# Where two token blocks take their first RMS norms from, and how far the attention's projections run ahead

## The chip, the core and the metric

The kernel runs on one core of one Trainium2 chip. The core has five queues of instructions that run beside each other: TensorE (PE in the profile, with its weight loads as PEld), VectorE (DVE), ScalarE (ACT), GpSimd (POOL) and SyncE (SP), which in this kernel issues all the DMA transfers. An engine works through its own queue in order and waits for others by semaphores. The metric is the device time of one execution in microseconds (us), the median over runs.

## The reference

One transformer layer, batch 1, 2048 tokens, width 1024, 16 heads of 64: an adaptive RMS norm, stick-breaking attention, a gated residual, a second adaptive norm, and a SwiGLU network of width 2816. Everything is float32. The part that the change touches is the first norm and what it feeds:

```python
def rms_norm(x, g):
    xf = x.astype(jnp.float32)
    y = xf * lax.rsqrt(jnp.mean(xf * xf, axis=-1, keepdims=True) + EPS)
    return (y * g.astype(jnp.float32)).astype(x.dtype)
...
    h = modulate(rms_norm(x, norm_g[i, 0]), sh_m, sc_m)
    y = stick_breaking_mixer(h, w_qkv, w_o)
...
    # in the mixer: causal blocks; softplus, a reversed running sum, exp
    qkv = (h @ w_qkv).reshape(b, s, 3, N_HEADS, HEAD_DIM)
    z = jnp.einsum('bthd,bshd->bhts', q[:, q0:end], k[:, :end]).astype(jnp.float32) * scale
    rest = lax.cumsum(jnp.where(mask, jax.nn.softplus(z), 0.0), axis=3, reverse=True)
    a = jnp.exp(jnp.where(mask, z - rest, -jnp.inf)).astype(v.dtype)
```

So each token needs one number, the reciprocal root of its mean square over the 1024 features; the features are then scaled, shifted and multiplied with the weights for Q, K and V.

## The kernel before

**Tiling.** The 2048 tokens are four blocks of 512 (b = 0 to 3), the 16 heads are eight pairs (p = 0 to 7), the 1024 features are KC = 8 chunks of 128. Products run in split precision: each operand is a high and a low float32r part, and one 128x128 by 128x512 product is three matmuls (`mm3`, L198 to L200). TensorE needs the normalised block with features on the partitions, `ht` (L415 to L423 write its two parts); it is also stored to DRAM (`h_s`), since later pairs load it from there.

**Projections.** A step is one (pair, block), in the order of `STEPS`: (0,0) and (1,0) first, woven together by hand, then (0,1), (0,2), (0,3), (1,1) and so on. Each later step is a generator `project` (L472) that computes K, then Q, then V (t = 1, 0, 2), eight products each, one per *slice*; with two empty slices a step has 26. After K and Q the result is split into two parts in a `qkn` buffer and moved by DMAs into `kt` and `qt`. The step (1,0) is *parked*: its K and Q are split into two `wraw` buffers and go by DMA to DRAM (`k_park`, `q_park`), to be fetched when pair 1 begins. There are two `wraw` buffers, three `qt`, seven `kt`, seven `v` and four `tmp` buffers, and three accumulator banks (`acc`) in PSUM.

**What sets the order.** The instructions of PE, ACT, DVE and POOL stand in the order in which the program text emits them; SP's DMAs are placed by the framework's scheduler. The attention runs in *slots*, four to a unit of (pair, head, query block, key block): in a slot PE multiplies one score tile `z`, ACT makes two sigmoids of an older one (L627, L629), DVE runs the product scan (L639, L644), POOL multiplies (L651), PE transposes (L661), and ACT and DVE split the result (L671, L677) for the product with V (L689). Between these stands a number of projection slices. `AHEAD` says how many slices are to be done by slot 11; the first slot comes after `AHEAD - EAGER` of them (30 and 12 make 18), and `RATE` spreads the rest of the 780 slices evenly over the attention's weighted slots.

**The first norm.** Block 0 is normalised by tokens: `x_load` puts 128 tokens a tile, ACT squares them with a sum (L189), DVE and POOL make the reciprocal root (L191, L193), DVE scales (L389), PE transposes four 128x128 pieces per chunk (`x_turn`, L395), ACT applies gain and shift. Blocks 1 to 3 come from `xt`, a copy of x that the host has laid out with features on the partitions (`cols_load`, L325: four tiles `xc` of two chunks). Block 1's mean squares are still taken by tokens, from a second load. Blocks 2 and 3 take them from the columns: ACT squares the four tiles (`cols_square`, L341), POOL and DVE add them up (L347, L349), PE sums over the partitions by four products with a column of ones (`cols_sum`, L355, into `xq`), DVE and POOL make the root (L359, L361). Four spread tiles (L369) are then transposed into a row over the tokens (`x_share`, L376), ACT copies it (`xv`, L381), and the columns are multiplied by it and the gain: even chunks on DVE (L404), odd ones on POOL (L408). `first_norm` (L435) does this three chunks ahead of the product that needs it. The table `X_AT` says at which (step, t, k) the pieces are emitted; `x_do` maps its words to functions.

Of the kernel before, what the change touches and what calls it, by code (L numbers as in the profile page):

```python
# [44 lines left out]
AHEAD = 3 * KC + 6  # L45
# [26 lines left out]

X_AT = {
    (2, 1, 1): [("load", 3)],
    (2, 1, 3): [("square", 2, 0)],
    (2, 1, 4): [("square", 2, 1), ("add", 2, 1)],
    (2, 1, 5): [("square", 2, 2)],
    (2, 1, 6): [("square", 2, 3), ("add", 2, 2)],
    (2, 1, 7): [("add", 2, 3)],
    (2, 0, 0): [("add", 2, 4)],  # L80
    (2, 0, 5): [("sum", 2)],
    (2, 0, 6): [("spread", 2)],
    (2, 2, 0): [("share", 2)],
    (2, 2, 3): [("square", 3, 0)],
    (2, 2, 5): [("square", 3, 1)],
    (2, 2, 7): [("add", 3, 1)],
    (3, 1, 0): [("square", 3, 2)],
    (3, 1, 2): [("add", 3, 2)],
    (3, 1, 3): [("square", 3, 3)],
    (3, 1, 5): [("add", 3, 3)],  # L90
    (3, 1, 6): [("add", 3, 4)],
    (3, 0, 1): [("sum", 3)],
    (3, 0, 2): [("spread", 3)],
    (3, 0, 6): [("share", 3)],
}

ON_GPSIMD = ((2, 1), (3, 1), (3, 2))
# [29 lines left out]
def hybrid_trunk_kernel(  # L127
# [25 lines left out]
    nc.vector.memset(lead, -0.5)  # L153
# [160 lines left out]
    x_pairs, x_squares, x_spreads = {}, {}, {}  # L314

    def x_load(b, i, tag="v"):
        tok = att.tile([P, D], F32, name=f"x{b}_{i}", tag=tag, bufs=BUFS[tag])
        r0 = b * BT + i * P
        nc.sync.dma_start(tok, x[r0 : r0 + P])
        x_tiles[b, i] = tok  # L320

    def cols_load(b, *which, tag="kt"):
        for m in which or range(KC // 2):
            cols = att.tile([P, 2, BT], F32, name=f"xc{b}_{m}", tag=tag, bufs=BUFS[tag])
            nc.sync.dma_start(cols, xt[b - 1, :, 2 * m : 2 * m + 2])  # L325
            x_pairs[b, m] = cols
            x_cols[b, 2 * m], x_cols[b, 2 * m + 1] = cols[:, 0], cols[:, 1]

    def x_square(b, i):
        junk = x_tiles[b, i]  # L330
        if b == 0:
            junk = x_norm[i] = att.tile([P, D], F32, name=f"xn0_{i}", tag="kt", bufs=BUFS["kt"])
        x_rstd[b, i] = rms_scale(att, x_tiles[b, i], f"n0_{b}_{i}", junk=junk)

    def cols_square(b, m):
        if m == 0 or (m == 2 and b == 2):
            both = att.tile([P, 2, 2, BT], F32, name=f"xs{b}_{m}", tag="qt", bufs=BUFS["qt"])
            x_squares.setdefault(b, []).extend([both[:, 0], both[:, 1]])
        elif m > 1 and b == 3:
            x_squares[b].append(x_squares[b][1])  # L340
        nc.scalar.activation(x_squares[b][m], x_pairs.pop((b, m)), AF.Square)  # L341

    def cols_add(b, m):
        total = x_squares[b][0]
        if m < KC // 2:
            engine = nc.gpsimd if (b, m) in ON_GPSIMD else nc.vector
            engine.tensor_tensor(total, total, x_squares[b][m], op=ALU.add)  # L347
        else:
            nc.vector.tensor_tensor(total[:, 0], total[:, 0], total[:, 1], op=ALU.add)  # L349

    def cols_sum(b):
        total = x_squares.pop(b)[0]
        ps = accps.tile([P, BT], F32, name=f"xq{b}", tag="acc")
        for i in range(4):
            nc.tensor.matmul(  # L355
                ps[:, i : i + 1], total[:, 0, i * P : (i + 1) * P], ones[:, 0:1], start=True, stop=True
            )
        ms = att.tile([P, 4], F32, name=f"xm{b}", tag="x_ms", bufs=1)
        nc.vector.tensor_scalar(ms, ps[:, :4], 1.0 / D, EPS, op0=ALU.mult, op1=ALU.add)  # L359
        rstd = att.tile([P, 4], F32, name=f"xd{b}", tag="x_rstd", bufs=1)  # L360
        nc.gpsimd.tensor_tensor(rstd, ms, lead[:, :4], op=ALU.pow)  # L361
        x_rstd[b] = rstd

    def x_spread(b, *which):
        if b not in x_spreads:
            x_spreads[b] = att.tile([P, 4, P], F32, name=f"xw{b}", tag="tmp", bufs=BUFS["tmp"])
        for i in which or range(4):
            rstd = x_rstd[b][:, i : i + 1] if b > 1 else x_rstd.pop((b, i))
            nc.vector.tensor_scalar(x_spreads[b][:, i], ones, rstd, None, op0=ALU.mult)  # L369

    def x_share(b):
        spread = x_spreads.pop(b)
        pool, tag = (tps, "t") if b < 2 else (accps, "acc")
        pt = pool.tile([P, BT], F32, name=f"xr{b}", tag=tag)
        for i in range(4):
            nc.tensor.transpose(pt[:, i * P : (i + 1) * P], spread[:, i], ident)  # L376
        if b == 1:
            x_row[b] = pt
            return
        x_row[b] = att.tile([P, BT], F32, name=f"xv{b}", tag="tmp", bufs=BUFS["tmp"])  # L380
        nc.scalar.copy(x_row[b], pt)  # L381

    x_do = {
        "load": cols_load, "square": cols_square, "add": cols_add, "sum": cols_sum,
# [3 lines left out]
    def x_scale(i):  # L388
# [380 lines left out]
    def turn_x(m):  # L769
        turned_x[m] = x_turn(m)  # L770
# [1033 lines left out]
```

## Time and profile before

| | us |
|---|---|
| median of 3 runs | 2848.14 (2847.87 to 2855.06) |
| the profiled execution's own time | 2851.93 |
| its span, first to last instruction | 2849.8 |
| PE busy in the span | 2802.1 (98%) |
| DVE busy | 2027.4 (71%) |
| ACT busy | 1633.5 (57%) |
| POOL busy | 1289.5 (45%) |

The span holds the whole program: an opening of some 65 us in which weights, x and the modulation arrive, the first projections and the start of the attention until about 150 us, the attention with its projections until about 1450 us, and then the output projection and the network. "Busy" of PE counts modelled ends of pipelined matmuls: two 128x512 matmuls of 0.39 us each that start 0.23 us apart run at full rate. The granted clock (PEclk) is the share of its full clock that TensorE was given. A row such as `L395 MATMUL xT<-begin,xn ... x4` reads: line 395, tile `xT` written from `begin` and `xn`, four of them. Names in lists of the program's order carry numbers of their buffers; in the profile these are left out.

### The profile page before, as it was taken

What the parts mean: (1) busy time and instruction counts of PE and PEld (TensorE: products, weight loads), DVE (VectorE), ACT (ScalarE), POOL (GpSimd) and SP (SyncE); (2) the same over time, 40 slices, a digit from 0 to 9 for tenths busy, and PEclk for the clock granted to TensorE, in tenths of its full rate; (3) what the DMA queues carried; (4) which work ended last, traced back from release to release, by engine and by line L of the source; (5) the groups of instructions that cost most, each with busy time, mean ns of one, the idle gap of its engine ahead of it and who ended that gap; (6) DMA issues with size and microseconds to landing.
All of it is one profiled execution on the core that took longest, in us unless ns stands there. A gap on an engine that the chain in (4) does not pass through costs nothing.

```text
span 2849.8 us, 41730 instructions
## 1 busy us (share of the span) xinstructions
PE 2802.1 (98%) x13809; PEld 2334.5 (82%) x13809; DVE 2027.4 (71%) x2828; ACT 1633.5 (57%) x3268; POOL 1289.5 (45%) x2033
## 2 busy tenths in 40 slices
PE   9799999999999999999999999999999999999999
PEld 6688888888888888887887888888888888888887
DVE  7688898888888888888866866655776655124366
ACT  5587777788787777877645533333433333322243
POOL 1575666666576655657410222222222222544454
PEclk9899999999999999999999999999999999999999
DMA  9765647657565545637289645334553335545575
GB/s 361 251 211 165 198 140 243 197 174 236 173 221 198 188 138 170 211 117 243 69 304 308 214 137 159 111 92 153 159 168 117 111 98 172 191 133 153 181 225 192
DMA packets 239209, 518.94 MB, mean 182 GB/s; under 512 B 22417, under 2 KB 108433, under 8 KB 222098
## 3 DMA queue, kind: packets, MB, share of 16 engines
q1 hardware_dynamic: 238994, 516.28, 55.8%
q8 instruction: 109, 1.79, 0.3%
q14 instruction: 106, 0.87, 0.1%
HBM read 348.95 MB, written 118.49 MB: 164 GB/s over the span
## 4 chain that ended last, share of the span: by engine, by line
PE 86%; DVE 4%; DMA 3%; issue 2%; ACT 2%; POOL 1%; SPq 0%; DVEq 0%; POOLq 0%; ACTq 0%
PE s L198 9%; PE s L200 9%; PE s L199 9%; PE z L610 8%; PE o L689 8%; PE t L661 8%; PE pj L198 5%; PE pj L199 5%; PE pj L200 5%; PE o L199 5%; PE o L198 5%; PE o L200 5%; PE y L200 1%; PE y L198 1%; PE y L199 1%
## 5 line engine op out<-in xcount | busy, mean ns | idle before, releaser
L651 POOL TENSOR_TENSOR a<-a,w 128x512 f32<-128x512 f32 (+3 forms) x640 | 622.7, 973 | 219.5 <-DVE w L644 129.0
L644 DVE TENSOR_TENSOR_SCAN w<-z,c,begin 128x512 f32<-128x512 f32 x384 | 489.6, 1279 | 83.4 <-ACT z L629 61.9
L198 PE MATMUL s<-r,l 128*128 128x512 f32 x1232 | 481.5, 391 | 1.2 <-DVE p L1535 0.7
L200 PE MATMUL s<-r,l 128*128 128x512 f32 x1232 | 479.6, 389 | 0.0
L199 PE MATMUL s<-r,l 128*128 128x512 f32 x1232 | 479.4, 389 | 0.0
L627 ACT ACTIVATE a<-z 128x512 f32<-128x512 f32 (+3 forms) x640 | 347.1, 542 | 168.1 <-PE z L610 137.7
L689 PE MATMUL o<-aT,v 128*128 128x512 f32 (+3 forms) x1280 | 385.0, 382 | 0.1
L677 DVE TENSOR_TENSOR aT<-t,aT 128x512 fp32r<-128x512 f32 (+3 forms) x640 | 359.1, 595 | 23.7 <-ACT aT L671 23.1
L610 PE MATMUL z<-kt,qt 128*128 128x512 f32 (+3 forms) x1280 | 364.8, 366 | 4.6 <-DVE w L639 4.6
L671 ACT CAST aT<-t 128x512 fp32r<-128x512 f32 (+3 forms) x640 | 313.9, 533 | 74.4 <-PE t L661 64.5
L629 ACT ACTIVATE z<-z 128x512 f32<-128x512 f32 (+3 forms) x640 | 344.8, 539 | 0.0
L1543 POOL TENSOR_TENSOR one<-p,p 128x512 f32<-128x512 f32 x44 | 70.6, 1604 | 574.6 <-issue 304.4
L198 PE MATMUL pj<-ht,w 128*128 128x512 f32 x768 | 310.2, 404 | 6.0 <-issue 1.4
L661 PE MATMUL t<-begin,a 128*128 128x128 f32 x2176 | 296.3, 274 | 13.5 <-DVE aT L677 12.3
L661 PEld LDWEIGHTS t<-begin,a 128*128 128x128 f32 x2176 | 256.2, 141 | 63.9 <-DVE aT L677 14.2
L199 PE MATMUL pj<-ht,w 128*128 128x512 f32 x768 | 302.8, 394 | 4.3 <-DVE ht L416 3.5
L200 PE MATMUL pj<-ht,w 128*128 128x512 f32 x768 | 302.7, 394 | 0.0
L198 PEld LDWEIGHTS s<-r,l 128*128 128x128 f32 x1232 | 231.3, 188 | 51.2 <-DVE p L1535 1.5
L200 PEld LDWEIGHTS s<-r,l 128*128 128x128 f32 x1232 | 231.3, 188 | 48.6 <-DVE l L1397 0.4
L199 PEld LDWEIGHTS s<-r,l 128*128 128x128 f32 x1232 | 231.3, 188 | 48.0 <-issue 0.5
L610 PEld LDWEIGHTS z<-kt,qt 128*128 128x128 f32 x1280 | 231.4, 189 | 42.5 <-DVE w L639 5.2
L639 DVE TENSOR_TENSOR_SCAN w<-z,begin 128x128 f32<-128x128 f32 (+3 forms) x256 | 208.8, 818 | 76.3 <-ACT z L629 65.4
(184 smaller groups left out, 4882.2 us busy)
## 6 DMA issues: line engine op xcount, KB each, us to landing
ht<-h_s SPq DMA_DIRECT2D x108, 1024.0 KB, 8.0
wi<-in_win SPq DMA_DIRECT2D x86, 512.0 KB, 4.0
qt<-qn SPq DMA_DIRECT2D x124, 256.0 KB, 4.8
ol_qt<-act_s SPq DMA_DIRECT2D x56, 512.0 KB, 3.7
act_s<-S SPq DMA_DIRECT2D x66, 256.0 KB, 3.9
br<-in_wout SPq DMA_DIRECT2D x66, 256.0 KB, 3.6
h_s<-ht SPq DMA_DIRECT2D x16, 1024.0 KB, 8.0
o_s<-os SPq DMA_DIRECT2D x128, 128.0 KB, 2.9
```

The lines of the kernel that those rows point to most:

```text
L198: nc.tensor.matmul(acc, lhs[0], rhs[0], start=first, stop=False, **kw)
L199: nc.tensor.matmul(acc, lhs[0], rhs[1], start=False, stop=False, **kw)
L200: nc.tensor.matmul(acc, lhs[1], rhs[0], start=False, stop=last, **kw)
L610: nc.tensor.matmul(z[:, :n], q[:, e, part, r * P : (r + 1) * P], k[:, e, :n], start=part == 0, stop=part == 1,)
L627: nc.scalar.activation(a[:, :n], z[:, :n], AF.Sigmoid, scale=QK_SCALE)
L629: nc.scalar.activation(z[:, :n], z[:, :n], AF.Sigmoid, scale=-QK_SCALE)
L644: nc.vector.tensor_tensor_scan(rest[:, rev], left[:, rev], begin[:, :BT][:, rev], initial=carries[r], op0=ALU.mult, op1=ALU.bypass,)
L651: nc.gpsimd.tensor_tensor(a[:, :n], a[:, :n], rest[:, 1 : n + 1], op=ALU.mult)
L661: nc.tensor.transpose(pt[:, rb * P : (rb + 1) * P], weighed[i, rb][:, j * P : (j + 1) * P], ident)
L671: nc.scalar.copy(hl[:, 0, t0:], pt[:, t0:])
L677: nc.vector.tensor_tensor(hl[:, 1, t0:], pt[:, t0:], f32(hl[:, 0, t0:]), op=ALU.subtract)
L689: nc.tensor.matmul(acc[:, t0:], lhs, hl[:, part, t0:], start=sc == qb and j == 0 and part == 0, stop=sc == 0 and j == 3 and part == 1,)
```

## The change

Block 2 is normalised by tokens in full, as block 0 is: its x is loaded by tokens into two `qt` buffers, squared (the squares themselves go to `wraw` buffers, of which only the sum is used), scaled on DVE, transposed chunk by chunk on PE into an accumulator bank, shifted and scaled on ACT into a `tmp` tile, and split by DVE in a copy and a subtraction. Block 3 keeps its columns, but takes its mean squares from a second load by tokens (into `v` buffers), as block 1 does; the spread is written into these tiles. `xt` holds blocks 1 and 3 only. The functions that add squares of columns are gone, and so is one constant (-0.5 in `lead`). `AHEAD` goes from 30 to 56 slices, so the first slot comes after 44 slices instead of 18. The diff, cut (lines of the opening that only carry another argument are left out):

```diff
-AHEAD = 3 * KC + 6
+AHEAD = 6 * KC + 8
...
+BY_FEATURES = (1, 3)
 X_AT = {
-    (2, 1, 1): [("load", 3)],
-    (2, 1, 3): [("square", 2, 0)],
-    (2, 1, 4): [("square", 2, 1), ("add", 2, 1)],
...
-    (2, 0, 5): [("sum", 2)],
-    (2, 0, 6): [("spread", 2)],
-    (2, 2, 0): [("share", 2)],
-    (2, 2, 3): [("square", 3, 0)],
...
-    (3, 0, 6): [("share", 3)],
+    (2, 1, 4): [("square", 2, 0)],
+    (2, 1, 5): [("square", 2, 1)],
+    (2, 1, 6): [("square", 2, 2)],
+    (2, 1, 7): [("square", 2, 3)],
+    (2, 0, 0): [("scale", 2, 0), ("load", 3)],
+    (2, 0, 1): [("scale", 2, 1)],
+    (2, 0, 2): [("scale", 2, 2)],
+    (2, 0, 3): [("scale", 2, 3)],
+    (3, 1, 0): [("cols", 3), ("square", 3, 0)],
+    (3, 1, 1): [("square", 3, 1)],
+    (3, 1, 2): [("square", 3, 2), ("spread", 3, 0)],
+    (3, 1, 3): [("square", 3, 3), ("spread", 3, 1)],
+    (3, 1, 4): [("spread", 3, 2)],
+    (3, 1, 5): [("spread", 3, 3)],
+    (3, 0, 1): [("share", 3)],
 }
-ON_GPSIMD = ((2, 1), (3, 1), (3, 2))
...
+    def x_load(b, *which, tag="v"):
+        for i in which or range(4):
+            r0 = b * BT + i * P
+            if b == 2:
+                if i % 2 == 0:
+                    x_places[b] = att.tile([P, 2, D], F32, name=f"x{b}_{i}", tag="qt", bufs=BUFS["qt"])
+                tok = x_places[b][:, i % 2]
+            else:
+                tok = att.tile([P, D], F32, name=f"x{b}_{i}", tag=tag, bufs=BUFS[tag])
+            nc.sync.dma_start(tok, x[r0 : r0 + P])
+            x_tiles[b, i] = tok
...
     def x_square(b, i):
         junk = x_tiles[b, i]
         if b == 0:
-            junk = x_norm[i] = att.tile([P, D], F32, name=f"xn0_{i}", tag="kt", bufs=BUFS["kt"])
+            junk = x_norm[b, i] = att.tile([P, D], F32, name=f"xn{b}_{i}", tag="kt", bufs=BUFS["kt"])
+        elif b == 2:
+            junk = att.tile([P, D], F32, name=f"xj{b}_{i}", tag="wraw", bufs=BUFS["wraw"])
         x_rstd[b, i] = rms_scale(att, x_tiles[b, i], f"n0_{b}_{i}", junk=junk)
-    def cols_square(b, m):
...
-    def cols_add(b, m):
...
-    def cols_sum(b):
...
+    def x_scale(b, i):
+        tok = x_tiles.pop((b, i))
+        if b > 0:
+            x_norm[b, i] = tok
+        nc.vector.tensor_scalar(x_norm[b, i], tok, x_rstd.pop((b, i)), None, op0=ALU.mult)
+
+    def x_spread(b, i):
+        nc.vector.tensor_scalar(x_tiles[b, i][:, :P], ones, x_rstd.pop((b, i)), None, op0=ALU.mult)
...
+    def x_turn(b, k):
+        pool, tag = (tps, "t") if b == 0 else (accps, "acc")
+        pt = pool.tile([P, BT], F32, name=f"xT{b}_{k}", tag=tag)
         for i in range(4):
             nc.tensor.transpose(
-                pt[:, i * P : (i + 1) * P], x_norm[i][:, k * P : (k + 1) * P], ident
+                pt[:, i * P : (i + 1) * P], x_norm[b, i][:, k * P : (k + 1) * P], ident
             )
...
     def scale_cols(b, k):
+        if b not in BY_FEATURES:
+            return
...
     def modulate(hl, b, k):
+        if b not in BY_FEATURES:
+            u = att.tile([P, BT], F32, name=f"hf{b}_{k}", tag="tmp", bufs=BUFS["tmp"])
+            nc.scalar.activation(u, x_turn(b, k), AF.Identity, bias=add, scale=gain)
+            nc.vector.tensor_copy(hl[:, 0], u)
+            nc.vector.tensor_tensor(hl[:, 1], u, f32(hl[:, 0]), op=ALU.subtract)
+            return
...
     row_done(6)
     low(5)
+    x_load(2, 0, 1)
     store(2)
...
-    cols_load(1, 3)
-    cols_load(2, 0, 1, tag="v")
+    x_load(2, 2, 3)
     products(0, 5)
...
-    cols_load(2, 2, tag="v")
...
-    cols_load(2, 3, tag="v")
```

### The order on the engines around it

ScalarE, in the step (0,1) while K is computed. Before, it squares the four column tiles of block 2 (`xc`) between the two casts of V (`v` of (0,0) and (1,0)) and the cast of K:

```order
L562 CAST v_0_722<-vt_0_717 128x8x64
L341 ACTIVATE xs_0_725<-xc_0_565 128x1024
L341 ACTIVATE xs_0_725<-xc_1_567 128x1024
L562 CAST v_0_740<-vt_0_735 128x8x64
L341 ACTIVATE xs_2_744<-xc_2_584 128x1024
L341 ACTIVATE xs_2_744<-xc_3_601 128x1024
L512 CAST kn_1_758<-pj_1_1_685 128x512
```

With the change, squares of block 2's tokens (`x_0_509` and `x_2_568` are the two `qt` buffers) stand in the same places; they write `xj`, in `wraw`:

```order
L540 CAST v_0_711<-vt_0_706 128x8x64
L183 ACTIVATE xj_0_717,n_2_0_ssq<-x_0_509 128x1024
L540 CAST v_0_732<-vt_0_727 128x8x64
L183 ACTIVATE xj_1_736,n_2_1_ssq<-x_0_509 128x1024
L183 ACTIVATE xj_2_746,n_2_2_ssq<-x_2_568 128x1024
L183 ACTIVATE xj_3_756,n_2_3_ssq<-x_2_568 128x1024
L490 CAST kn_1_766<-pj_1_1_682 128x512
```

The squares moved neither up nor down in the queue; what they read and write is another buffer.

ScalarE again, with the change, in the step (0,2) while K is computed: the shifted chunks 3 to 7 of block 2 (`hf`) alternate with squares of block 3's tokens, where before no such pairs stood:

```order
L387 ACTIVATE hf_3_885<-xT_3_886,mod,g_eff 128x512
L183 ACTIVATE x_0_776,n_3_0_ssq<-x_0_776 128x1024
L387 ACTIVATE hf_4_913<-xT_4_914,mod,g_eff 128x512
L183 ACTIVATE x_1_778,n_3_1_ssq<-x_1_778 128x1024
L387 ACTIVATE hf_5_931<-xT_5_932,mod,g_eff 128x512
L183 ACTIVATE x_2_780,n_3_2_ssq<-x_2_780 128x1024
L387 ACTIVATE hf_6_952<-xT_6_953,mod,g_eff 128x512
L183 ACTIVATE x_3_782,n_3_3_ssq<-x_3_782 128x1024
L387 ACTIVATE hf_7_971<-xT_7_972,mod,g_eff 128x512
```

Before, block 3's squares stood among the first slots' sigmoids instead.

TensorE in V of the step (0,1). Before, the attention's first score tile comes after two of the eight products:

```order
L198 MATMUL pj_1_2_814<-ht_1_0_603,w_2_317 128x512
L199 MATMUL pj_1_2_814<-ht_1_0_603,w_2_317 128x512
L200 MATMUL pj_1_2_814<-ht_1_0_603,w_2_317 128x512
L610 MATMUL z_0_828<-kt_0_655,qt_0_666 128x128 x2
L198 MATMUL pj_1_2_814<-ht_1_1_648,w_2_317 128x512
```

With the change the first transposes of block 2 stand there, and the first score tile comes 26 slices later, in V of (0,2):

```order
L194 MATMUL pj_1_2_819<-ht_1_0_600,w_2_317 128x512
L366 MATMUL xT_0_828<-begin,x_0_509 128x128 x2
L366 MATMUL xT_0_828<-begin,x_2_568 128x128 x2
L192 MATMUL pj_1_2_819<-ht_1_1_645,w_2_317 128x512
```

All products of (0,2) but the last six of V moved ahead of the attention.

More of the change, by code (lines that the diff above doesn't have):

```diff
@@ L343, in cols_add @@
-    def cols_add(b, m):
[L344 to L349, printed above, removed]
-    def cols_sum(b):
[L352 to L369, printed above, removed]
+    def x_scale(b, i):
[3 more added lines that the diff above has]
+        nc.vector.tensor_scalar(x_norm[b, i], tok, x_rstd.pop((b, i)), None, op0=ALU.mult)
@@ L375, in x_share @@
         for i in range(4):
[L376 to L381, printed above, removed]
+            tok = x_tiles.pop((b, i))
+            nc.tensor.transpose(pt[:, i * P : (i + 1) * P], tok[:, :P], ident)
+        x_row[b] = pt
+        if b > 1:
+            x_row[b] = tok[:, BT:]
+            nc.scalar.copy(x_row[b], pt)
     x_do = {
[L384 removed]
+        "load": x_load, "cols": cols_load, "square": x_square, "scale": x_scale,
         "spread": x_spread, "share": x_share,
     }
[L388 to L393 removed]
+    def x_turn(b, k):
+        pool, tag = (tps, "t") if b == 0 else (accps, "acc")
+        pt = pool.tile([P, BT], F32, name=f"xT{b}_{k}", tag=tag)
         for i in range(4):
             nc.tensor.transpose(
[L396 removed]
+                pt[:, i * P : (i + 1) * P], x_norm[b, i][:, k * P : (k + 1) * P], ident
             )
@@ L903, in hybrid_trunk_kernel @@
     row_load(5)
-    x_load(1, 2, "wraw")
+    x_load(1, 2, tag="wraw")
     row_load(6)
-    x_load(1, 3, "wraw")
+    x_load(1, 3, tag="wraw")
     cols_load(1, 0)
```

52 lines of the change are left out of this document (12 added, 40 removed).

## The prediction

> **What bounds the kernel now.** I read the busy time of the engines by stages first, then TensorE's list of waits, then the timelines of PE, ACT and SP around each wait. The columns after the stretch are its length, then busy time (and count) of PE, PEld, DVE, ACT, POOL, the granted clock, the DMA share and GB/s.
>
> ```profile
> 0.00:65.00 65.00, 60.84 (x275) 45.95 (x276) 50.68 (x102) 38.06 (x59) 6.63 (x15) 1.00 0.97 377
> ...
> 110.00:150.00 40.00, 34.07 (x180) 28.09 (x180) 32.24 (x48) 27.74 (x60) 27.96 (x45) 0.96 0.47 145
> 150.00:1450.00 1300.00, 1285.77 (x7040) 1087.52 (x7039) 1111.85 (x1466) 1010.96 (x2133) 806.70 (x1670) 1.00 0.57 185
> ```
>
> ```profile
> 65.00:85.00 20.00, 16.56 (x73) 13.16 (x71) 10.88 (x16) 6.19 (x9) 6.44 (x5) 0.91 0.97 321
> 85.00:110.00 25.00, 15.56 (x53) 11.22 (x53) 17.18 (x19) 18.72 (x36) 14.45 (x16) 0.73 0.99 361
> ```
>
> TensorE is the bound nearly everywhere: in the 1300 us of the attention it stands still for 14.2, with DVE next at 86%. Only between 65 and 150 us does it lose much. I count as lost what is idle, and of the busy time the share of the clock that was not granted: 3.4 + 16.56 x 0.09 = 4.9 us in 65 to 85, 9.4 + 15.56 x 0.27 = 13.6 in 85 to 110, 5.9 + 34.07 x 0.04 = 7.3 in 110 to 150. That is **25.9 us**, and it is all that this change can win back, since the matmuls themselves stay. PE's waits there:
>
> ```profile
> PE t L661 <- DVE aT L677: 5.9, 4, 2.3
> PE z L610 <- DVE w L639: 4.6, 1, 4.6
> PE pj L199 <- DVE ht L416: 3.5, 2, 2.3
> PE xq L355 <- DVE xs L349: 3.1, 2, 2.7
> ```
>
> `xq` and `ht` are the norms of blocks 2 and 3; the wait for `w` goes back to them too, because ScalarE's queue stood before a square of block 3 whose columns had not landed, and later before one that waited for POOL's sum:
>
> ```profile
> 85.34 1.06 ACT L341 ACTIVATE xs<-xc 128x1024 f32<-128x1024 f32 x1 [4.08 <-DMA xc<-in_xt]
> ...
> 103.65 1.06 ACT L341 ACTIVATE xs<-xc 128x1024 f32<-128x1024 f32 x1 [4.44 <-POOL w L624]
> ```
>
> A stop costs more than its length. The last matmul of K in step (0,1), the first wait, and what follows it:
>
> ```profile
> 69.55 0.39 PE L200 MATMUL pj<-ht,w 128*128 128x512 f32 x1
> 72.62 1.06 PE L355 MATMUL xq<-ones,xs 128*128 128x1 f32 x8 [2.68 <-DVE xs L349]
> 73.55 0.78 PE L198 MATMUL pj<-ht,w 128*128 128x512 f32 x1
> 74.12 0.63 PE L199 MATMUL pj<-ht,w 128*128 128x512 f32 x1
> ...
> 76.68 0.52 PE L199 MATMUL pj<-ht,w 128*128 128x512 f32 x1
> 77.04 0.40 PE L200 MATMUL pj<-ht,w 128*128 128x512 f32 x1
> 77.28 0.60 PE L376 MATMUL xr<-begin,xw 128*128 128x128 f32 x4
> 77.63 0.48 PE L198 MATMUL pj<-ht,w 128*128 128x512 f32 x1
> ```
>
> At full rate matmuls start 0.23 us apart (77.04 to 77.28), so a slice of three takes 0.69; after the stop they start 0.43 apart for some eight matmuls, 1.6 us lost on top.
>
> **The change, part by part.**
>
> *Work on PE (a).* Four transposes move the clock on by 0.35 us (77.28 to 77.63), the four products of `xq` by 0.93 (72.62 to 73.55). Block 2 now needs 8 x 0.35 = 2.8 us of transposes; both `xq` (1.86) and block 2's `xr` (0.35) go. Net **+0.6 us**, on the path, since PE is the bound.
>
> *The squares of block 2 (b).* They stand in the same places of ScalarE's queue, and their tokens are issued no later than the columns were. But their by-product goes to a `wraw` buffer, and both `wraw` buffers hold the parked K and Q of step (1,0) until SP has sent these to DRAM. So the first square waits for `k_park` to land and the third for `q_park`:
>
> ```profile
> 69.43 0.45 SPq L524 DMA_DIRECT2D k_park<-kn  x1
> 69.98 0.65 SPq L538 DMA_DIRECT2D q_park<-qn  x1
> ```
>
> ```profile
> k_park<-kn SPq DMA_DIRECT2D x1, 512.0 KB, 4.7
> q_park<-qn SPq DMA_DIRECT2D x1, 512.0 KB, 5.4
> ```
>
> The last number is the time from issue to landing: 74.1 and 75.4 us. The DMAs ahead of them carry as many bytes as before. Before, ScalarE's squares of block 2 began at 64.3 us:
>
> ```profile
> 64.30 2.01 ACT L341 ACTIVATE xs<-xc 128x1024 f32<-128x1024 f32 x2
> ```
>
> Now the queue stands still until 74.1, and behind the square wait a cast of V, the other squares and the cast of K. The durations, as mean ns of one:
>
> ```profile
> L189 ACT ACTIVATE x<-x 128x1024 f32<-128x1024 f32 x4 | 4.2, 1052 | 0.0
> L774 ACT ACTIVATE hf<-xT,mod,g_eff 128x512 f32<-128x512 f32 x8 | 6.2, 778 | 13.4 <-DVE g_eff L740 12.4 <-PE xT L395 0.9
> L512 ACT CAST kn<-pj 128x512 fp32r<-128x512 f32 x4 | 2.4, 593 | 3.3 <-PE pj L200 2.6 <-DMA kt<-kn 0.7
> L562 ACT CAST v<-vt 128x512 fp32r<-128x512 f32 x4 | 2.3, 578 | 2.0 <-PE vt L558 2.0
> ```
>
> ```profile
> L389 DVE TENSOR_SCALAR xn<-x,n_rstd 128x1024 f32<-128x1024 f32 x4 | 3.0, 749 | 0.0
> L789 DVE TENSOR_TENSOR ht<-hf,ht 128x512 fp32r<-128x512 f32 x8 | 5.5, 686 | 1.6 <-ACT ht L785 1.6
> L513 DVE TENSOR_TENSOR kn<-pj,kn 128x512 fp32r<-128x512 f32 x4 | 2.7, 684 | 0.1
> ```
>
> From 74.1: four squares and a cast of V, 4 x 1.05 + 0.58, to 78.9; the cast of K to 79.5; DVE's half of K, ahead of the scalings in its queue, to 80.2; four scalings, 4 x 0.75, to 83.2. The roots on POOL fit in between. PE meanwhile ends K at 69.8, does Q (8 x 0.69) and two products of V, and stands at block 2's first transposes from 76.7. It waits 6.5 us, and the slow clock takes 1.6 more: **8.1 us**. The bounds are 0, should the parked tiles leave early, and 10 with both clock penalties of the old stops.
>
> *K of step (0,2) (c).* No slot runs beside it now. Behind `xT` 3 ScalarE has five `hf` and four squares of block 3's tokens, 5 x 0.78 + 4 x 1.05 = 8.1 us; with 0.35 for the transposes before it, a copy on DVE (0.37, half of the 1024-wide scaling, an estimate), the subtraction (0.69) and the last slice (0.69) the chain takes 10.2, PE's own work 8 x 0.69 + 5 x 0.35 = 7.3. That is **2.9 us** lost. The tokens must be there: ScalarE asks for the first at about 92 (83.2, six slices and two `xT`, 1.6 of slow clock, V's transposes). From the landing of `q_park` (75.4) to that of the first column tile of block 3 (85.3, above) three 1 MB stores and 0.5 MB passed, 2.8 us a MB. With the change 5.5 MB lie ahead of the end of the first token tile: 75.4 + 15.5 = 90.9, and each next 1.4 later. They fit, narrowly. Behind them `qt` of (0,1), which now waits for block 2's last transposes, and block 3's columns pass in time for V of (0,2), 10 us further on.
>
> *The first slots (d).* Block 3's norm now stands beside slots 0 to 8, where block 2's stood: 13.6 us lost in 85 to 110. Of these the two waits of ScalarE for block 3's squares, 4.1 and 4.4, go. 5.1 stay. Pair 1's first weights are now issued behind two of block 3's stores, which wait for POOL, and ScalarE's split of them stands in K of (0,3): I add 1.4, an estimate. **6.5 us**, bounds 1 and 13.6.
>
> *The slots after (e).* In 110 to 150 block 3's norm ran beside slots 9 on; now no norm does. But pair 1's weights and its first projections come five units sooner. Bounds 0 and the old 7.3; nearer the old, since the scans and sigmoids of short diagonal tiles are still there: **4.5 us**.
>
> *Fewer slices in the attention (f).* 26 slices, 26 x 0.69 = 17.9 us of matmuls, leave the attention for the stage ahead of it. This costs nothing where PE is the bound: then slots get shorter. Where DVE's chain (86% busy) sets the pace, the slot stays as long. Bounds 0 and 17.9; with PE idle for only 1.1% I take the lower part: **4 us**.
>
> The extra 2 MB of tokens lie in a queue that has room from 110 us on (0.47). Sum: 0.6 + 8.1 + 2.9 + 6.5 + 4.5 + 4 = 26.6 us lost in place of 25.9, **+0.7 us**. Against the profiled execution's 2851.9 (span 2849.8 and 2.1 around it) that is 2852.6; that execution lies 3.8 above the median of the runs, 2848.1, so the median becomes 2848.8.
>
> One term looks different by a rule. DVE's subtraction of 0.75 us took 2.51 beside one of POOL's sums of squares:
>
> ```profile
> 100.81 2.81 POOL L347 TENSOR_TENSOR xs<-xs 128x1024 f32<-128x1024 f32 x1
> ```
>
> ```profile
> 101.66 2.51 DVE L416 SCALAR_TENSOR_TENSOR ht<-xc,mod,ht 128x512 fp32r<-128x512 f32 x1
> ```
>
> The Trainium skill, SBUF — State Buffer, section "Who interferes with whom", says that a DVE instruction with two SBUF inputs and a GpSimd instruction that reads SBUF take turns on a shared port pair, the later one blocked to the end. The row agrees (101.66 + 2.51 ends 0.55 after POOL's 103.62). By it d falls by another 1.8, as the sums are gone, and the time would be 2847.0.
>
> **The rivals.**
>
> *Slower: the attention misses its filler.* If DVE's chain sets the slots, f is 17.9 and not 4: 2848.8 + 13.9 = 2862.7. For it speaks DVE's 86% over 1300 us, against it PE's 99% in the same row. It decides from f = 11.8 on (8.5 us over 2848.1).
>
> *Slower: block 3's tokens come late.* ScalarE's queue holds `hf` behind each square, so PE stops in K of (0,2) for as long as the tokens are late, and the columns, behind them and behind a `qt` that waits for the last transposes, hold V's norms up once more. At 3.9 us a MB, an estimate, instead of 2.8 the first tokens land at 75.4 + 5.5 x 3.9 = 96.9, 5 us after they are asked for, and the columns cost some 4 more: 2848.8 + 9 = 2857.8. It decides from about 8 us in all. For it: the margin is 1 us. Against: any delay in b gives the queue the same time.
>
> *Faster: the attention starts clean.* With all the squares gone from the slots, d, e and f fall to 2, 1 and 1 from 15 in all: 2848.8 - 11 = 2837.8. For it: PE was gapless where little norm work ran, and not where more did:
>
> ```profile
> 115.00:120.00 5.00, 5.00 (x29) 4.11 (x29) 3.86 (x10) 2.27 (x5) 2.75 (x10) 1.00 0.24 95
> ...
> 130.00:135.00 5.00, 2.73 (x17) 2.07 (x16) 5.00 (x6) 3.70 (x10) 4.52 (x5) 1.00 0.38 157
> ```
>
> Against it: most of the waiting in the slots was for the scan chain (`aT`, above). If only b's wait is missing, the time is 2840.7, still near no change.
>
> **How the numbers follow.** A measurement of this kernel can tell about 0.3%, 8.5 us, from no change. No change, with b and c in place of the old stops: 0.50. Missing filler: 0.16. Late tokens: 0.16. Clean start: 0.18. So faster 0.18, within 0.50, slower 0.32. The likeliest case has 2840 to 2857, the 8.5 us that define it; the range reaches to 2838, the clean start, and to 2863, the missing filler. The predicted time is **2849 us**.
>
> **What would show it.** In the changed profile: a wait of ScalarE at the square of block 2 (L183) until `k_park` lands near 74, and one of PE of 6 to 7 us at the first `xT` of block 2 (b); `hf` and squares back to back on ScalarE in K of (0,2), with no wait for `x` (c); a loss of PE in the first slots well under 13.6 us (d); PE busy 98.5 to 99% of the attention, and the attention as a whole shorter by about 14 us of the 17.9 that left it (f). A PE that never stops before 100 us, or an attention as long as before, would make it wrong.

## The result, and the profile after

The changed kernel takes 2842.85 us (median of 9 runs, 2839.84 to 2848.03), the kernel before, run beside it, 2851.80 (9 runs, 2847.87 to 2856.61). The ratio is **0.9973, 95% interval 0.9963 to 0.9983**: faster, by 9 us in the medians and 8 by the ratio. The forecast was 2849 and no change.

| | before | after |
|---|---|---|
| span of the profiled execution, us | 2849.8 | 2837.4 |
| PE busy in the span | 2802.1 | 2798.4 |
| PE's loss in 65 to 85 us | 4.9 | 7.8 |
| in 85 to 110 | 13.6 | 1.7 |
| in 110 to 150 | 7.3 | 7.9 |
| PE idle in 150 to 1400 | 13.5 | 14.5 |

Loss is counted as in the prediction, idle time and the part of the busy time that the clock was not granted. The stages of the profile after, in the columns of the first fence of the prediction:

```profile
65.00:85.00 20.00, 14.65 (x55) 11.07 (x54) 7.27 (x16) 7.26 (x13) 2.19 (x4) 0.83 1.00 360
85.00:110.00 25.00, 23.27 (x115) 17.79 (x114) 13.55 (x29) 13.70 (x25) 6.12 (x7) 1.00 0.98 343
110.00:150.00 40.00, 35.29 (x173) 27.99 (x171) 27.61 (x38) 30.13 (x67) 29.19 (x45) 0.91 0.89 300
150.00:1400.00 1250.00, 1235.46 (x6828) 1047.82 (x6827) 1080.69 (x1399) 990.96 (x2089) 799.01 (x1671) 1.00 0.56 180
```

The stretch from 65 to 150 us loses 17.4 us in place of 25.9; the attention gives 1.0 back. The first transpose of the second norm, for which PE waits in both kernels, is a mark at the end of the attention. Before and after:

```profile
1443.96 0.33 PE L1082 MATMUL h2T<-begin,x1n 128*128 128x128 f32 x1 [0.58 <-DVE x1n L1075]
```

```profile
1435.93 0.33 PE L1059 MATMUL h2T<-begin,x1n 128*128 128x128 f32 x1 [0.57 <-DVE x1n L1052]
```

It stands 8.0 us earlier. 8.5 won less 1.0 and less 0.6 for the transposes makes 6.9, so some 1 us is left open. The spans differ by 12.4: between 1500 and 1700 us the profiled execution of before loses 4.8 us, at an `h2T` that waited 2.5, that of after 0.4, those of the experiments 0.4 to 2.1. That the medians differ by 9.0 speaks for the mark, not the spans.

PE's waits in 85 to 150 us, after:

```profile
PE pj L193 <- POOL w L602: 2.5, 2, 2.0
PE pj L193 <- DVE ht L394: 1.1, 1, 1.1
PE vt L536 <- ACT vT L530: 0.9, 2, 0.7
PE t L639 <- DVE aT L655: 0.9, 2, 0.6
```

Gone are `z <- w` (4.6), both `xq` and most of the 5.9 for `aT`. The first row is new. Its releaser is a semaphore event of POOL next to a memset of 0.1 us; what PE waited for ends just before, the low part of an odd chunk of block 3 (115.98 + 1.27 = 117.25). POOL's timeline, and PE's:

```profile
114.74 1.28 POOL L380 TENSOR_TENSOR xc<-xc,x 128x512 f32<-128x512 f32 x1
115.98 1.27 POOL L401 TENSOR_TENSOR ht<-xc,ht 128x512 fp32r<-128x512 f32 x1
117.18 0.10 POOL L602 MEMSET w<- 128x1 f32 x1
```

```profile
117.30 0.50 PE L193 MATMUL pj<-ht,w 128*128 128x512 f32 x1 [2.00 <-POOL w L602]
```

So the stops that are left beside the first slots stand at block 3's second half, whose odd chunks pass POOL twice.

A single profiled execution of this kernel is good to about 5 us only: in some of them, before 65 us, where PE does nearly the same work in all these kernels, the clock is lower and PE loses 9 to 11 us in place of 4 to 5 (last section). Times below are therefore medians against runs of before on the same chip, and profiles are used for the place of a loss, from 65 us on. The profiles of e1, e3, e9, e10, e11 and e12 are of this kind. Their PE comes to 65 us some 5 us late, so a wait there for a transfer can be shorter than it is in the others.

### The profile page after: what moved, and what is told of

Same layout as the page of the kernel before. It is cut to its first block, busy times and chain, and to the rows that moved or that the text cites. A ratio compares the mean times of both kernels' runs of the same rounds, so it can differ in the third digit from the quotient of the medians.

```text
span 2837.4 us, 41791 instructions
## 1 busy us (share of the span) xinstructions
PE 2798.4 (99%) x13821; PEld 2331.6 (82%) x13821; DVE 2021.1 (71%) x2833; ACT 1632.1 (58%) x3271; POOL 1281.6 (45%) x2032
## 4 chain that ended last, share of the span: by engine, by line
PE 89%; DVE 3%; DMA 3%; issue 2%; ACT 2%; POOL 1%; SPq 1%; DVEq 0%; POOLq 0%; ACTq 0%
PE s L192 9%; PE s L194 9%; PE s L193 9%; PE z L588 8%; PE o L667 8%; PE t L639 8%; PE pj L192 6%; PE pj L194 6%; PE pj L193 6%; PE o L193 5%; PE o L192 5%; PE o L194 5%; PE y L194 1%; PE y L192 1%; PE y L193 1%
```

## The experiments

### Each half alone: e1_norms_alone, e2_lead_alone

e1 is the changed kernel with the old lead, e2 the kernel before with the new one.

```diff
-AHEAD = 6 * KC + 8
+AHEAD = 3 * KC + 6
```

```diff
-AHEAD = 3 * KC + 6
+AHEAD = 6 * KC + 8
```

> The changed norms with the old lead (AHEAD = 30, first slot after 18 slices). Theory: the gain comes from taking the norms out of the first slots, which the lead does; the wait for the parked K stays (7 to 8 us lost in 65 to 85 us) and block 3's five hf and four squares now stand beside the first slots again, so 85 to 150 us loses 14 to 20 and the time is that of the kernel before: ratio 0.998 to 1.002. Rival (the form of the norm alone brings it, since no square waits for columns to land): ratio 0.996 to 0.998, 85 to 150 us loses 10 or less.

> The kernel before with the new lead alone (AHEAD = 56, first slot after 44 slices). Theory (the lead brings it): 65 to 85 us loses 4.9 as before, 85 to 110 loses 6 to 9 in place of 13.6 because the squares still wait for block 3's columns, 110 to 150 loses 1 to 3; ratio 0.995 to 0.998. Rival (the norm's form brings it): ratio 0.999 to 1.001, the stops merely stand elsewhere. A third reading, that fewer slices in the attention cost something there, would show PE idle for over 18 us in 150 to 1450 us in place of 14.2.

e1: 2840.28, **ratio 0.9964 (0.9951 to 0.9976)**. The theory fell, and its rival (the form of the norm) is right: the new norms without the lead gain as much as with it. e2: 2845.15, ratio 0.9977 (0.9968 to 0.9986): the lead alone gains 6.6 us, which these runs do not tell apart from the whole change, so the halves do not add. PE's waits in 85 to 150 us, of e1 and then of e2:

```profile
PE t L639 <- DVE aT L655: 5.9, 4, 2.3
PE xT L366 <- DVE x L340: 0.7, 2, 0.3
```

```profile
PE vt L558 <- ACT vT L552: 7.1, 2, 6.9
PE pj L199 <- DVE ht L416: 3.8, 2, 2.8
PE pj L199 <- POOL w L624: 2.4, 2, 1.9
PE t L661 <- DVE aT L677: 0.4, 1, 0.4
```

e1 has the 5.9 us for `aT` of the kernel before, to the tenth, and 0.2 for POOL; the changed kernel has POOL's 2.5 and 0.9 for `aT`. In 110 to 150 us e1 loses 7.6, the changed kernel 7.9. One thing that was expected of e1 is missing: 65 to 85 us loses 2.6, not 7 to 8. ScalarE's first square still waits, but 4.4 us, and PE stands at block 2's first transposes for 3.0 us in all; as this is one of the executions with the lower clock in the opening, it does not show that the old lead saves this. e2 keeps the old form's stop: ScalarE stands before a square of block 3 whose columns have not landed, with V's copy behind it, and no slot is near:

```profile
85.97 1.06 ACT L341 ACTIVATE xs<-xc 128x1024 f32<-128x1024 f32 x1 [4.49 <-DMA xc<-in_xt]
```

So e2 loses 5.5 us in 65 to 85, 12.8 in 85 to 110 (6 to 9 were expected) and 7.3 in 110 to 150 (1 to 3). That is 25.6 in place of the 25.9 of before, and PE's idle time in 150 to 1400 us falls by 0.3 only: the waits show hardly any of the 6.6 us. The mark at the end of the attention stands 3.5 us earlier than before:

```profile
1440.44 0.33 PE L1082 MATMUL h2T<-begin,x1n 128*128 128x128 f32 x1 [0.58 <-DVE x1n L1075]
```

Where the lead alone gains is therefore open.

### Which block's norm, and whether the place of the squares is enough: e10_block3_only, e9_late_squares

e10 is the kernel before with block 3's means from tokens, e9 the kernel before with its own column squares further back. First e10 (`mean` is `x_square`, `tokens` loads into `kt`):

```diff
-    (2, 1, 1): [("load", 3)],
...
-    (2, 0, 0): [("add", 2, 4)],
+    (2, 0, 0): [("add", 2, 4), ("tokens", 3)],
...
-    (2, 2, 3): [("square", 3, 0)],
...
-    (3, 0, 6): [("share", 3)],
+    (3, 1, 0): [("load", 3), ("mean", 3, 0)],
+    (3, 1, 1): [("mean", 3, 1)],
+    (3, 1, 2): [("mean", 3, 2), ("spread", 3, 0)],
+    (3, 1, 3): [("mean", 3, 3), ("spread", 3, 1)],
...
+    (3, 0, 1): [("share", 3)],
```

And e9:

```diff
-    (2, 2, 3): [("square", 3, 0)],
-    (2, 2, 5): [("square", 3, 1)],
...
+    (3, 1, 0): [("square", 3, 0)],
+    (3, 1, 1): [("square", 3, 1)],
+    (3, 1, 2): [("add", 3, 1)],
+    (3, 1, 3): [("square", 3, 2)],
...
+    (3, 1, 7): [("add", 3, 4)],
```

> The kernel before, lead 30, with block 3's means alone taken by tokens (loaded into kt buffers, its columns then into v buffers); block 2 is left by features. Theory: block 3's form carries the gain of the new norms and block 2's costs some: 65 to 85 us loses 4.9 as before, 85 to 110 loses 2 to 5, time 2837 to 2842, no more than e1_norms_alone (2840.3). Rival: block 2's form carries it, and this is at 2847 to 2851. Third: block 3's columns wait for v buffers until block 2's columns are used, and a new wait stands in K of (0,3): above 2845 with that wait named.

> The kernel before, with block 3's four column squares and their adds stood five or more slices further back, in K of step (0,2), where the changed kernel has its squares; lead, loads and bytes as before. Theory: most of the 13.6 us lost in 85 to 110 us came from ScalarE's queue standing before squares of columns that had not landed (4.1 us) or whose sum POOL had not done (4.4), ahead of V's copy; so this alone loses 4 to 8 there and the time is 2842 to 2847. Rival: the norm's chain then ends too late for block 3's first chunks, PE waits there instead, and the time is 2849 or more.

e10: 2842.53, **ratio 0.9970 (0.9960 to 0.9980)**, the gain of the whole change with block 2 and the lead untouched. It loses 2.7 us in 65 to 85, 5.4 in 85 to 110 (before: 13.6) and 7.6 in 110 to 150:

```profile
85.00:110.00 25.00, 21.10 (x98) 16.52 (x97) 20.75 (x35) 22.64 (x50) 15.37 (x30) 0.93 1.01 363
```

e9: 2850.18, 0.9998 (0.9989 to 1.0006): no gain, the rival, though its runs spread over 12 us (2844.57 to 2856.61). Its waits in 85 to 150 us:

```profile
PE t L661 <- DVE aT L677: 5.1, 3, 2.3
PE pj L199 <- DVE ht L416: 3.2, 2, 2.3
PE xq L355 <- DVE xs L349: 2.4, 1, 2.4
PE pj L198 <- ACT ht L415: 1.1, 1, 1.1
```

The landing is no longer waited for, but now PE waits for the sum over features, which passes POOL and DVE before its product can be made. The old form had two ends in this stretch, its columns early or its sum late; means by tokens need neither. So at the old lead block 3's new form is enough for the gain, and the place of the squares is not. It is not the only way to it, as e2 shows.

### The wait for the parked tiles: e3_junk_elsewhere, e5_early_tokens, e8_lead30_early, e11_fewer_bytes

e3 changes one line of the changed kernel; e5 is e3 with the second piece, e8 is e5 with `AHEAD = 3 * KC + 6`, and e11 is e5 with the third piece. e11 leaves out seven eighths of what block 1 stores of its `ht`, and pairs 1 to 7 read block 0's in its place, so its result is not the layer's; it serves to price the bytes.

```diff
-            junk = att.tile([P, D], F32, name=f"xj{b}_{i}", tag="wraw", bufs=BUFS["wraw"])
+            junk = att.tile([P, D], mybir.dt.bfloat16, name=f"xj{b}_{i}", tag="a", bufs=BUFS["a"])
```

```diff
+    (2, 1, 2): [("load", 3)],
...
-    (2, 0, 0): [("scale", 2, 0), ("load", 3)],
+    (2, 0, 0): [("scale", 2, 0)],
```

```diff
+            if b == 1:
+                out_of = out_of[0][:16], out_of[1][:16]
...
-            nc.sync.dma_start(f32(ht), h_s[b][:, 2 * k2 : 2 * k2 + 2])
+            nc.sync.dma_start(f32(ht), h_s[0 if b == 1 else b][:, 2 * k2 : 2 * k2 + 2])
```

> The changed kernel with the squares of block 2 written as bfloat16 into buffers of the attention's `a`, which are free until the first slot; nothing else is changed. Theory: the wait for the parked K and Q is the whole of the loss in 65 to 85 us (7.8), so the first square starts at 65 to 67 us instead of 71.5 and the time is 5 to 8 us below the changed kernel: ratio to before 0.9945 to 0.9960. Rival: the queue of DMAs, not the buffer, sets what follows, and the wait comes back at block 3's tokens or columns: under 2 us gained, ratio 0.9965 to 0.9975.

> As e3_junk_elsewhere, and block 3's tokens are asked for 14 slices earlier (two products into K of step (0,1)), which puts them ahead of kt of (0,1), v_park and one store of h_s. Theory: in e3 the wait for the parked tiles came back as ScalarE's wait of 3.9 us for block 3's tokens; with them there, 65 to 110 us loses under 4 us in place of 7 to 9.5, the 7 us at 110 to 130 stay, and the time is 2835 to 2839. Rival: the DMA engines are full from 65 to 115 us, so what is moved ahead only makes something else late (kt, qt or block 3's columns): 2839 to 2842 with a new wait named there.

> As e5_early_tokens, with the old lead of 30. Theory: the wait in 65 to 85 us and the lead are independent, so this lies as far below e1_norms_alone (2840.3) as e5 lies below the changed kernel, 4 to 7 us: 2834 to 2837. Rival: with the first slots from the V of (0,1) on, kt and qt of (0,1), now behind the tokens, are wanted early, PE waits at z for them and the gain goes: 2839 to 2843.

> As e5_early_tokens, but the four 1 MB stores of block 1's h are cut to an eighth of their partitions, and pairs 1 to 7 read block 0's h in place of block 1's (the attention of that block is then computed from the wrong tokens). Theory: the DMA engines, full from 65 to 115 us, are what every one of these waits goes back to; 3.5 MB less there is worth 10 us of their time, ScalarE's wait of 12.3 us for qt (and PE's of 8.0 at z behind it) is gone, and the time is 2830 to 2836. Rival: qt waits for its buffers, which hold block 2's tokens until their last transposes, not for bytes: the wait stays over 5 us and the time at 2841 to 2845.

e3: 2840.74, ratio 0.9963 (0.9950 to 0.9977), 2 us under the changed kernel by medians and not told apart from it; 5 to 8 us were expected. The wait for the parked K is gone (65 to 85 us loses 0.7), 85 to 110 us loses 6.3 in place of 1.7, and the rival is there, in ScalarE's queue and behind it on PE:

```profile
89.84 1.06 ACT L183 ACTIVATE x<-x 128x1024 f32<-128x1024 f32 x1 [3.87 <-DMA x<-in_x]
```

```profile
91.70 0.66 PE L366 MATMUL xT<-begin,x 128*128 128x128 f32 x4 [3.19 <-ACT hf L387]
```

e5 fetches these tokens earlier: 2845.11, 0.9980 (0.9971 to 0.9989), no gain again, if not a loss. Little is lost at block 2 and the tokens now (1.1 us in 65 to 85, 1.7 in 85 to 95), but Q of (0,1) reaches `qt` late, its `qkn` buffer stays taken, and ScalarE cannot write the next Q. e8 is e5 with the first slots early; there PE needs that `qt` itself: 2848.53, 0.9996 (0.9987 to 1.0005). ScalarE of e5 and PE's wait behind it, then PE's wait in e8:

```profile
107.89 0.59 ACT L491 CAST qn<-pj 128x512 fp32r<-128x512 f32 x1 [12.28 <-DMA qt<-qn]
```

```profile
PE z L589 <- DVE w L618: 8.0, 1, 8.0
```

```profile
PE z L589 <- DMA qt<-qn: 12.1, 1, 12.1
```

Taking bytes away helps: e11, 3.5 MB less and otherwise e5, takes **2837.30, ratio 0.9955 (0.9943 to 0.9967)**, 7.8 us under e5 by medians and 7 by the ratios. In the profiles the wait for `qt` falls from 12.28 to 7.89, PE's wait at `z` from 8.0 to 2.4:

```profile
105.90 0.59 ACT L493 CAST qn<-pj 128x512 fp32r<-128x512 f32 x1 [7.89 <-DMA qt<-qn]
```

```profile
PE z L591 <- DVE w L620: 2.4, 1, 2.4
```

This fits the reading that in this stretch the DMA engines set the pace (their share in 65 to 85 and in 85 to 110 us is 0.96 to 1.02 in these four), and that a wait that is taken away comes back at the next transfer that is due. The two profiles show less of it than the times. Of the 4.4 us by which the wait for `qt` is shorter, 2.4 are ScalarE's own delay (it comes to this cast at 98.0 us in place of 95.6, after an opening at the lower clock) and 2.0 an earlier landing; the slowest DMA of `qt` takes 12.0 us from issue to landing, in e5 11.6. That is far from the 10 us that 3.5 MB cost at 350 GB/s, an estimate from the rates above, and the wait stays over 5 us, as the rival said. Where the rest of e11's gain arises is open.

### The stop at POOL: e6_low_on_dve

```diff
-            eng = nc.gpsimd if b == NB - 1 else nc.vector
+            eng = nc.vector
```

> The changed kernel with the low parts of block 3's four odd chunks subtracted on DVE in place of POOL; nothing else. Theory: PE's stops at 115 to 123 us (2.0, 1.1 and 0.5 us, and the slow clock behind them) are POOL's, which has two passes of 1.3 to 1.7 us for each odd chunk and the slots' products between; without one of the two the loss in 110 to 130 falls from 7.1 to 2 to 4 us and the time is 2838 to 2841. Rival: DVE's extra 0.7 to 1.5 us a chunk stands ahead of its scans, PE waits for aT again as it did before the change (5.9 us there), and nothing is gained: 2842 to 2846.

2841.57, ratio 0.9976 (0.9965 to 0.9987), where the changed kernel has 0.9973: nothing gained, the rival. Its waits in 85 to 150 us:

```profile
PE t L639 <- DVE aT L655: 3.5, 3, 2.3
PE pj L193 <- DVE ht L394: 2.3, 1, 2.3
```

POOL's stop is gone, and the wait for `aT` is back with one for DVE. The loss in 110 to 150 us is 7.6, as in the changed kernel (7.9) and in e1 (7.6): three lists of waits with nearly one sum. That the one wait stands in for the other is not shown by this: e6 gives the work to DVE, which also runs the scans and makes `aT`, and more work on DVE can lengthen that wait by itself.

### The lead: e7_lead_42, e13_lead_46, e14_lead_47, e12_lead_48, e4_lead_68

All five are the changed kernel with another number for `AHEAD`.

> The changed kernel with a lead of 42 slices, half way between 30 and 56. Theory: with the new norms the lead only trades PE's waits for aT (5.9 us at 30, 0.9 at 56) for waits for POOL's chunks (0.2 at 30, 2.5 at 56), so the time lies with the other two: 2839 to 2844, and 110 to 150 us loses 5 to 9. Rival 1: an optimum between, with neither wait, 2834 to 2838. Rival 2: both kinds together, above 2846.

> The changed kernel with a lead of 46; in SyncE's queue the qt of (0,3) stands behind the first load of h for (1,1), as at 30, 42 and 56. Theory (the order of that queue decides): no wait of PE for ht from h_s over 1.5 us, 2836 to 2844. Rival (the lead's number of slices decides, with 48 and 68 on the far side of a limit): near 48, 2848 to 2856.

> The changed kernel with a lead of 47; the qt of (0,3) now stands ahead of the first load of h for (1,1) and of one DMA of kt of (1,0), as at 48 and 68. Theory (the order decides): PE waits 3 to 6 us for ht from h_s near 165 us, loses 5 to 8 us more than usual in 400 to 800 us, and the time is 2848 to 2858, 8 or more above the lead of 46. Rival: one slice changes nothing, both within 3 us of each other.

> The changed kernel with a lead of 48 slices. Theory: PE's waits for aT (2.0 us in 85 to 160 us at a lead of 42, 0.9 at 56) and for POOL's and DVE's chunks of block 3 (2.0 and 0.5 at 42, 2.5 and 1.1 at 56) change slowly with the lead, so the time lies between those of 42 (2836.8) and 56 (2842.9): 2836 to 2842. Rival: 42 was low by chance, and 48 is at 2842 to 2846 like 56.

> The changed kernel with a lead of 68 slices in place of 56 (first slot after 56, in the middle of K of step (0,3)): 12 more slices, 8.3 us of matmuls, leave the attention. Theory: the attention lacks no filler, and the stops at 115 to 123 us come from block 3's chunks on POOL standing beside slots; the loss in 110 to 150 us falls from 7.9 to 3 to 5, PE idle in the attention stays at 14 to 16: ratio to before 0.9955 to 0.997. Rival 1: the attention misses its filler and PE idle there grows by 4 to 8 us: ratio 0.998 to 1.001. Rival 2: K of (0,3) is bound by POOL's and ScalarE's chain for odd chunks without any slot, and the loss stays: ratio 0.997 to 0.998.

| lead | median, us | ratio to before (95%) | PE's waits for `ht` from `h_s` | loss in 110 to 150 | PE idle in 150 to 1400 |
|---|---|---|---|---|---|
| 30 (e1) | 2840.28 | 0.9964 (0.9951 to 0.9976) | none | 7.6 | 12.9 |
| 42 (e7) | 2836.80 | 0.9959 (0.9947 to 0.9971) | none | 4.0 | 12.9 |
| 46 (e13) | 2844.40 | 0.9980 (0.9972 to 0.9989) | 2.8 | 8.9 | 14.4 |
| 47 (e14) | 2844.88 | 0.9983 (0.9974 to 0.9992) | 2.3 | 9.8 | 15.1 |
| 48 (e12) | 2856.22 | 1.0018 (1.0009 to 1.0027) | 7.1 | 6.6 | 22.0 |
| 56 (the change) | 2842.85 | 0.9973 (0.9963 to 0.9983) | 1.0 | 7.9 | 14.5 |
| 68 (e4) | 2859.35 | 1.0033 (1.0020 to 1.0045) | 5.6 | 16.2 | 17.5 |

The lead has no slope. 42 has the lowest median, 6 us under the changed kernel by medians and 4 by the ratios, but the intervals overlap, and with that of the old lead (e1) more so. There the waits for `aT` and POOL are both small (2.0 and 2.0), the optimum between that e7 had as a rival. 48 and 68 take longer than any reading allowed. A new wait stands out in them, for loads of h: at 68 one of 5.6 us, at 48 one of 4.3 near 168 us and one of 2.9 between 400 and 500. Pair 1's first loads stand in SP's queue behind DMAs that wait for a `qt` buffer. SP at 68, and PE's wait there:

```profile
129.87 2.55 SPq L437 DMA_DIRECT2D kt<-k_park  x4
136.93 3.04 SPq L523 DMA_DIRECT2D qt<-qn  x4
140.02 1.19 SPq L447 DMA_DIRECT2D v<-v_park  x1
141.25 2.58 SPq L407 DMA_DIRECT2D ht<-h_s  x4
```

```profile
148.53 0.79 PE L192 MATMUL pj<-ht,w 128*128 128x512 f32 x1 [5.60 <-DMA ht<-h_s]
```

SP issues nothing from 132.4 to 136.9. e13 and e14 were to show that it is the place of this one `qt`, that of (0,3), against the first load of h that decides. That fell: 46 and 47 stand on two sides of the change of order and take the same time, both with a wait of 2 to 3 us. In both, and at 48, the other loads are issued at 161 us, behind the `qt` fetched from `q_park`; at 42 they are issued at 155, since that `qt` does not wait, and at 56 at 148 and 149, ahead of it. That this second `qt` decides fits all the traces and was not tried. Why 48 is 11 us slower than 47 is only half found: 6.9 us more idle in the attention, of which 1.6 lie in 150 to 200 us, 2.7 in 400 to 500 and 2.0 in 600 to 700, at no single wait.

### Block 3's form with the best lead: e15_block3_lead_42

e10 with `AHEAD = 42`.

> Block 3's means by tokens, block 2 by features, lead 42 (as e10_block3_only with 12 slices more). Theory: the lead of 42 is worth as much here as with both norms changed (2836.8 against 2840.3), so 2836 to 2841, and block 2's form matters little. Rival: the gain at 42 needs block 2's tokens, which stop TensorE ahead of the first slots and let DVE and POOL run ahead: 2842 or more.

2839.70, ratio 0.9963 (0.9951 to 0.9976): as expected, and not told apart from e7 or e10. So no need of block 2's new form is shown at this lead either. But the profiles differ: e15 loses 10.4 us in 85 to 110, where e7 loses 1.4, and its mark at the end of the attention stands 4.2 us later.

## Why the prediction was wrong

The sum said +0.7 us and no change; the runs give 9 us less. Of the six terms two were badly sized and one a little, all three too high. The prediction also took 0.3%, 8.5 us, as what a measurement can tell from no change; nine runs of each kernel gave an interval of 0.1% to either side.

- **(b) was right in mechanism and place; its size agrees by luck.** Forecast: ScalarE's first square of block 2 waits for `k_park` to land, 8.1 us lost. Measured: 7.8 lost in 65 to 85 us.

```profile
71.48 1.06 ACT L183 ACTIVATE xj<-x 128x1024 f32<-128x1024 f32 x1 [7.07 <-issue]
```

```profile
65.53 1.05 SPq L502 DMA_DIRECT2D k_park<-kn  x1
66.69 1.51 SPq L516 DMA_DIRECT2D q_park<-qn  x1
```

```profile
k_park<-kn SPq DMA_DIRECT2D x1, 512.0 KB, 5.9
```

  65.53 + 5.9 = 71.4, where the square starts. 74.1 was forecast: the four DMAs of `qt` ahead of it took SP 4.4 us to issue, not 8.1. So the squares began 2.6 us earlier than forecast. But PE came earlier too: the prediction took 69.55 us for the end of K, while the product there is Q's fifth (the table has `sum` at (2, 0, 5)), so K ended some 3.4 us before. PE stood from 73.4 us, not from 76.7:

```profile
72.96 0.39 PE L194 MATMUL pj<-ht,w 128*128 128x512 f32 x1
78.14 0.47 PE L366 MATMUL xT<-begin,x 128*128 128x128 f32 x1 [4.78 <-DVE x L340]
```

  The two errors nearly cancel. PE waited 5.3 us for the four transposes in place of 6.5, and the slow clock behind them took 2.5 in place of 1.6. Nor are the 7.8 a price that can be saved by itself; e3 and e5 show most of them come back.
- **(c), 2.9 forecast, measured 1.7.** ScalarE has `hf` and squares back to back from 89.3 to 96.9, with no wait for a token, as forecast. The narrow margin of block 3's tokens was real: without b's delay they are late by 3.9 us (e3), which the text had as "any delay in b gives the queue the same time". The 3.9 us a MB of the rival with late tokens stands in no row; the 343 to 360 GB/s of 65 to 110 us make 2.9 to 3.1.
- **(d) came out near its size.** 6.5 forecast, 6.8 measured in 110 to 130 us. But it is not made of what the sum had: no wait of PE for pair 1's weights shows, and the loss stands at block 3's second half, 3.6 us of waits for chunks from POOL and DVE and 2.7 of slow clock.
- **(e) is the step that failed most**: "nearer the old, since the scans and sigmoids of short diagonal tiles are still there: 4.5 us". Measured 0.6 in 130 to 150 us. The scans are still there, but PE's wait for `aT` is 0.9 us in place of 5.9. Counted in one piece, 110 to 150 us loses 7.9 (the parts give 7.4, as the clock is rounded), where the prediction added (d) and (e) to 11.0. That PE's waits for `aT` and for block 3's chunks share slots, so that the scans catch up while PE stands at a chunk, would explain it: with the low parts moved to DVE the wait for `aT` returns (0.9 to 3.5, e6), with the old lead it is at its old 5.9 and the chunks' is gone (e1), and both lose 7.6. It is not shown, since e6 loads DVE itself, and the sum is not fixed: with a lead of 42 both waits are at 2.0 and the loss is 4.0.
- **(f) was taken too large**: 4 us for 26 slices fewer in the attention, measured 1.0 (13.5 to 14.5 us idle), none in e2 (13.2). The slots got shorter: from the first score tile to the mark are 1364.9 us before (from 79.11) and 1329.9 after (from 106.02). That is 34.9 less, more than the 17.9 us of matmuls that left, since stops went from this stretch too; the prediction's sign was about 14. The rival with 17.9 us is refuted for 56. A lead of 68 does cost, 5.6 us of it at loads that SP issues late.
- **(a)**, 0.6 us, is under what these runs can tell.

In sum, (c), (d) with (e), and (f) were 1.2 + 3.1 + 3.0 = 7.3 us too high and (b) 0.3: 19.0 us lost in place of 26.6, 6.9 under the old 25.9, where the mark says 8.0 and the medians 9.0. What wins, the prediction had in (d): ScalarE's two waits for block 3's squares, 8.5 us, go. e10 has this without the lead and block 2's new form and gains as much as the whole change. The prediction set too much against it. That the lead alone gains nearly as much (e2) was not foreseen, and its cause is open.

The Trainium skill, SBUF — State Buffer, section "Who interferes with whom", gave 2847.0, on the ground that POOL's sums are gone. The rows after agree with the rule, but the conclusion did not follow: other POOL instructions now stand there. DVE's subtraction of 0.75 us took 1.57 and 1.42:

```profile
117.72 1.57 DVE L394 SCALAR_TENSOR_TENSOR ht<-xc,mod,ht 128x512 fp32r<-128x512 f32 x1
119.55 1.42 DVE L394 SCALAR_TENSOR_TENSOR ht<-xc,mod,ht 128x512 fp32r<-128x512 f32 x1
```

```profile
117.36 1.38 POOL L629 TENSOR_TENSOR a<-a,w 128x512 f32<-128x512 f32 x1
118.71 1.72 POOL L380 TENSOR_TENSOR xc<-xc,x 128x512 f32<-128x512 f32 x1
```

Each ends 0.54 to 0.55 us after the POOL instruction that ran when it began (119.29 after 118.74, 120.97 after 120.43), as the row of before did.

## What to carry to other kernels

Waits that a profile lists for one stretch need not add up, and one that is taken away can come back elsewhere: price a stretch by its whole loss, and test one wait by moving it and looking at that loss again, with work that does not load another engine of the same chain. When two terms of a forecast agree with the result, check their parts too; (b) agreed because two errors of some 3 us cancelled. With the DMA engines at a share of 0.96 to 1.02, asking for a transfer earlier gained nothing here (e5, e8) and fewer bytes did (e11). A lead of one stage over another moves each DMA's place in SP's queue, which is issued in order, so it has to be tried at several values; four slices more than the best cost 7.6 us by medians here.

## What the runs showed of the hardware

**The clock in the opening differs from run to run.** Up to 60 us these kernels issue nearly the same work on PE, and in all 17 profiled executions PE stands still for some 1.3 us between 15 and 25 us. Yet in six of them (e1, e3, e9, e10, e11 and e12) PE was then granted half its clock for 10 to 13 us between 20 and 35 us. The changed kernel, then e1:

```profile
25.00:30.00 5.00, 5.00 (x25) 3.92 (x24) 4.52 (x8) 4.49 (x6) 0.00 (x0) 1.00 1.03 409
```

```profile
25.00:30.00 5.00, 5.00 (x18) 4.11 (x18) 1.09 (x2) 0.00 (x0) 0.00 (x0) 0.50 1.02 409
```

That is 5 to 7 us of PE time, more than half of the 8 us over which the nine runs of the changed kernel spread. The Trainium skill, TensorE: Matmul & The Clock Gate, Part 1, states that the gate looks at PE's activity in a window that runs freely and does not begin with the kernel; that would make the same short stop cost nothing in one run and half the clock in the next, and the two rows agree with it, though no run here shows the window.
